# State-space layer of a hybrid encoder: phasor tables transposed to [state group, step], and the carry between runs worked out once for the two groups of a pair

## The chip, the cores and the metric

One core of one Trainium2 chip runs the whole kernel. The metric is the device time of one execution in microseconds (us), the median of three timed runs. A difference of about 0.2% (4.4 us here) is what a measurement of this kernel can tell from no change. The profile is of one more execution, taken by the hardware profiler.

## The reference, cut to what matters

The kernel computes one encoder layer of 2048 positions and 1024 channels: an input projection, three mixers side by side (state space, Fourier, windowed attention), an output projection, and a gated feed-forward part. The change lies in the state-space mixer alone:

```python
lam_bar = jnp.exp(lam * dt)                                  # per direction, group and state
b_bar = ((lam_bar - 1.0) / lam)[..., None] * b
for d, rev in ((0, False), (1, True)):
    bu = complex(einsum(u, b_bar[d].real), einsum(u, b_bar[d].imag))
    h[d] = associative_scan(a * left + right, (lam_bar[d], bu), reverse=rev, axis=1)
y = einsum(h.real, c_re) - einsum(h.imag, c_im) + d_skip * u
y = gelu(y); y = y * sigmoid(y @ w_glu)
```

There are 24 channel groups of 16 channels, each with 64 complex states and two directions.

## The kernel before, in words

**The state-space mixer.** Two groups make a pair, so there are 12 pairs. The sequence is cut into 256 blocks of 8 positions. Within a block the work is done by matmuls; across the 256 blocks a complex recurrence runs. It is made real by phasors: block values are rotated by the angle that has built up since the start of a *run* of 16 blocks, and then a real scan with the magnitudes (`rho`) suffices. So 256 blocks are 16 runs of 16 blocks, and 512 columns hold the two directions of a group. Real and imaginary parts lie in the two halves of the 128 partitions.

Four tables hold cosine and sine of the angles: `t1c` and `t1s` for the step inside a run, `t2c` and `t2s` for the run. `s5_consts` (L730) builds them as [16 steps, 48 columns], a column being one group and direction; `phasors` (L840) fills them by doubling, the first pair of tables on VectorE and the second on GpSimd. L832 multiplies the two sine tables by a sign. A multiplication of 512 columns by a table takes it with `bt(tsel(table))`: 16 entries for the inner dimension, 48 elements apart, used again for each of the 16 runs.

`s5_pair` (L861) prepares a pair: it builds matrices on VectorE (the first two pairs) or GpSimd, transposes them on TensorE, copies magnitudes into `RT` (L905), and puts two entries, one per group, into the queue `s5q`. `s5_chain` (L953) takes an entry and works it to the end. `N_CH` = 3 copies of it run at once, so three groups are in flight. Of one group it does:

1. two TensorE products into two PSUM banks `XA` and `XB` (fp32), a copy of magnitudes to `rx` on ScalarE (L979);
2. two multiplications of 128x512 by `t1c` and `t1s` (L980, L981), an addition, and a scan of 512 columns (L984);
3. the carry between runs (L986 to L1001) on 32 columns, the ends of the 32 runs: nine short VectorE instructions, among them a scan of 32 columns, and twice a TensorE product with the permutation `perm`, which swaps the halves of the partitions;
4. a second scan of 512 columns with the carries added in (L1002), two multiplications by the tables (L1003, L1004);
5. five TensorE products that make the output `y`, a ScalarE copy, and a DMA that stores it to `yd`.

When both groups of a pair are stored, its place among three prepared pairs (`N_SL`) comes free and `f_yd[b]` is set.

**What sets the order.** The program is written out by a planner (`Sched`, L121). Each part is a generator that asks for an engine with an estimated cost (`tt` at L277: 0.07 + 0.00105 per column, whatever the access pattern; `scan` at L302, `act` at L272, `mm` at L318). The planner always emits the instruction that can start earliest on its own clock, with a priority for ties. Each engine then runs its instructions strictly in the emitted order. Since all go through helpers, the profile's lines are those of the helpers: L277 two-operand arithmetic, L302 scans, L291 three-operand arithmetic, L318 matmuls, L272 ScalarE, L267 DMA. Parts outside the mixer are let in by futures: the Fourier weights by `f_yd[0]`, the preparation of the output weights by `f_yd[4]`, the remaining query tiles (`zrest`, 24 f16 matmuls of 128x512 each) by `f_yd[6]`, modulation rows (L446, L444) by `f_yd[7]`, gated linear unit and attention by `f_yd[10]`. The output projection needs all three mixers; the feed-forward part follows it.

Of the kernel before, what the change touches and what calls it, by code (L numbers as in the profile page):

```python
# [16 lines left out]
P = 128  # L17
# [26 lines left out]
S5_MUL = "V"  # L44
# [158 lines left out]
class Builder:  # L203
# [214 lines left out]
    def setup(self):  # L418
        A = self.A
        self.ones, self.ccol = self.const([P, P]), self.const([P, 8])  # L420
        self.bada, self.gains = self.const([P, 48]), self.const([P, 4, 8])
        yield from self.mset(0, self.ones, 1.0 / 1024)
        t = yield from self.dma(0, self.ccol, A["c_col"])
        t = yield from self.dma(0, self.bada, A["b_ada"])
        t = yield from self.dma(0, self.gains, A["gains"])
        self.f_cst.set(t)
        self.par, self.sgn = self.const([P, 3, 48]), self.const([P, 1])
# [302 lines left out]
    def s5_consts(self):  # L730
# [98 lines left out]
        for f in ends:  # L829
            t = max(t, (yield ("w", f)))  # L830
# [30 lines left out]
    def s5_pair(self, b, t, slots):  # L861
# [44 lines left out]
        left = [2, 0.0]  # L906
        for g in range(2):
            self.s5q.append((b, g, max(tp, tr), f_u, f_m, wt, U, RT, M0, Vf, Vs, left, slots))
            f, self.f_s5q = self.f_s5q, Fut()
            f.set(0)  # L910
        self.s5n -= 1
        if self.s5n == 0:
            self.f_s5q.set(0)
# [37 lines left out]
        done.set(t1)  # L951

    def s5_chain(self):  # L953
        PE = self.PE
        v4 = lambda a: a.rearrange("p (d a b) -> p d a b", d=2, a=16)
        v3 = lambda a: a.rearrange("p (d a) -> p d a", d=2)
        fl = lambda a: a.rearrange("p d a -> p (d a)")
        bt = lambda a: a.unsqueeze(2).to_broadcast([P, 2, 16, 16])
        M, ADD, SUB = ALU.mult, ALU.add, ALU.subtract
        while True:  # L960
            while not self.s5q:
                if self.s5n == 0:
                    return
                yield ("w", self.f_s5q)
            b, g, t, f_u, f_m, wt, U, RT, M0, Vf, Vs, left, slots = self.s5q.pop(0)
            t = max(t, (yield ("w", f_u)))
            s0 = 4 * b + 2 * g
            tsel = lambda tab: tab[:, :, s0:s0 + 2].rearrange("p b d -> p d b")
            tb_ = yield ("acq", self.bank["s"], 2)
            XA, XB = self.ps("s"), self.ps("s")  # L970
            rhs = (U[:, g, :], U[:, g, ::-1])
            ops = [(XX[:, d * 256:d * 256 + 256], wt[:, 2 * g + d, o:o + 128], rhs[d], True, True)
                   for XX, o in ((XA, 0), (XB, 64)) for d in range(2)]
            ta = yield from self.mm(max(t, tb_), ops[:2])
            tb = yield from self.mm(max(t, tb_), ops[2:])
            t12, rxs = self.u([2, 512]), self.u([768])
            gg, tt_ = t12[:, 0], t12[:, 1]
            rx, sc = rxs[:, 0:512], self.shape(rxs[:, 512:768], [8, 2, 16])
            tx = yield from self.act(t, v4(rx), bt(RT[:, 0, 2 * g:2 * g + 2]), AF.Copy)  # L979
# [3 lines left out]
            t = yield from self.tt(max(ta, tb), gg, gg, tt_, ADD, eng=S5_ADD)  # L983
            t = yield from self.scan(max(t, tx), tt_, rx, gg)  # L984

            pe_ = XA  # L986
            ends = v4(tt_)[:, :, :, 15]
            c2, s2 = tsel(self.t2c), tsel(self.t2s)
            tc_ = yield from self.tt(t, sc[:, 1], ends, c2, M)
            t = yield from self.mm(t, [(pe_[:, 0:32], self.perm, ends, True, True)])  # L990
            t = yield from self.tt(t, sc[:, 0], v3(pe_[:, 0:32]), s2, M)
            t = yield from self.tt(t, sc[:, 1], sc[:, 1], sc[:, 0], ADD)
            t = yield from self.scan(t, fl(sc[:, 2]), fl(RT[:, 1, 2 * g:2 * g + 2]), fl(sc[:, 1]))
            k1 = sc[:, 4, :, 1:16]
            tk = yield from self.tt(t, k1, sc[:, 2, :, 0:15], c2[:, :, 1:16], M)
            t = yield from self.mm(t, [(pe_[:, 64:96], self.perm, fl(sc[:, 2]), True, True)])
            t = yield from self.tt(t, sc[:, 3, :, 1:16], v3(pe_[:, 64:96])[:, :, 0:15], s2[:, :, 1:16], M)
            t = yield from self.tt(t, k1, k1, sc[:, 3, :, 1:16], SUB)
            t = yield from self.tt(t, k1, k1, self.rho[:, 0, s0:s0 + 2].unsqueeze(2).to_broadcast([P, 2, 15]), M)
            g4 = v4(gg)  # L1000
            t = yield from self.tt(t, g4[:, :, 1:16, 0], g4[:, :, 1:16, 0], k1, ADD)  # L1001
            t = yield from self.scan(t, tt_, rx, gg)  # L1002
            t1 = yield from self.tt(t, v4(rx), v4(tt_), bt(tsel(self.t1s)), M, eng=S5_MUL)  # L1003
            t = yield from self.tt(t, v4(gg), v4(tt_), bt(tsel(self.t1c)), M)  # L1004
            t = max(t, t1)
            tm = yield ("w", f_m)
            y = XA[:, 0:256]
            ops = [(y, M0[:, g, :], U[:, g, :], True, False)]
            for j, pp in ((0, gg), (1, rx)):
                ops.append((y[:, 1:256], Vf[:, 2 * g, 16:144] if j == 0 else Vs[:, 2 * g], pp[:, 0:255], False, False))  # L1010
                ops.append((y[:, 0:255], Vf[:, 2 * g + 1, 0:128] if j == 0 else Vs[:, 2 * g + 1],
                            pp[:, 256:511][:, ::-1], False, j == 1))
            t = yield from self.mm(max(t, tm), ops)
            t = yield from self.act(t, U[:, g], y, AF.Copy)
            self.free(t, XA)
            r = slice(16 * (2 * b + g), 16 * (2 * b + g) + 16)
            t = yield from self.dma(t, self.yd[r].rearrange("c t k -> t c k"), U[:, g])
            left[0] -= 1
            left[1] = max(left[1], t)
            if left[0] == 0:  # L1020
                slots.give(left[1])
                self.f_yd[b].set(left[1])


    def f_evac(self, t, ps, dst, done):
# [1088 lines left out]
```

## Time and profile before

| | |
|---|---|
| median of three runs | 2199.02 us (2198.71 to 2199.77) |
| the profiled execution | 2203.73 us, of which the span of instructions is 2202.0 us |
| mean granted TensorE clock | 0.955 |
| state-space stage: first table multiplication to last output | about 157 to 427 us |
| attention: first and last score row (L1327) | 500.2 and 870.1 us |

In the profile, PE is TensorE's matmul, PEld its weight load, DVE is VectorE, ACT ScalarE, POOL GpSimd and SP the queue from which DMAs are issued. A group's row gives line, engine, operation, output and inputs by name (`u` is any buffer in the chip's working memory, `ps` a PSUM bank, `c` a constant, `st` attention statistics), shapes, count, then busy time in us and mean duration of one in ns, then the engine's idle time just before them and what ended it. Durations of instructions that follow each other overlap a little, so a group's busy time is less than count times mean. A row of windows gives a stretch, its length, each engine's busy time with its count, then the granted TensorE clock, the DMA share and GB/s. A row of waits gives the waiting engine and line, what it waited for, the total in us, the number of times and the longest.

### The profile page before, as it was taken

How to read it: one execution, taken by the hardware profiler on the slowest of the kernel's cores; microseconds unless marked ns; L12 is line 12 of the kernel's file. 1: busy time of each engine (PE TensorE's matmuls, PEld its weight loads, DVE VectorE, ACT ScalarE, POOL GpSimd, SP SyncE). 2: the span in 40 equal slices, each digit the busy share in tenths (PEclk: the TensorE clock that was granted, in tenths of full speed). 3: DMA queues.
4: the chain of work that ended last, by engine and by line, in shares of the span. 5: the costliest groups of instructions: out<-in, count | busy, mean ns of one | idle time of the engine just before them, and what ended most of it. 6: DMA issues, size and time to landing. Idle time of an engine off the chain costs nothing.

```text
span 2202.0 us, 27575 instructions
## 1 busy us (share of the span) xinstructions
PE 2004.0 (91%) x10120; PEld 1001.0 (45%) x10120; DVE 1597.4 (73%) x2400; ACT 984.3 (45%) x1670; POOL 246.6 (11%) x310
## 2 busy tenths in 40 slices
PE   6778787889998858898999999999999999999997
PEld 2335565445454425443444444444444444444445
DVE  8999999886676584879988885565656665446456
ACT  3623233336576556556655553444444433222321
POOL 0565545020100000000000000000000000011002
PEclk9988898999999979799999999999999999999998
DMA  9351123673735273335655557565656494538533
GB/s 367 105 190 60 41 93 135 210 267 124 241 118 173 95 244 103 114 127 210 244 205 186 187 187 300 195 220 203 219 201 224 144 343 143 182 119 292 188 110 110
DMA packets 206667, 397.31 MB, mean 180 GB/s; under 512 B 19522, under 2 KB 111939, under 8 KB 206531
## 3 DMA queue, kind: packets, MB, share of 16 engines
q1 hardware_dynamic: 206530, 395.55, 52.2%
q8 instruction: 79, 1.29, 0.2%
q14 instruction: 58, 0.47, 0.1%
HBM read 258.93 MB, written 134.98 MB: 179 GB/s over the span
## 4 chain that ended last, share of the span: by engine, by line
PE 61%; DVE 25%; ACT 5%; issue 4%; DMA 3%; POOL 1%; SPq 1%; DVEq 0%; POOLq 0%; ACTq 0%
PE ps L318 61%; DVE u L277 12%; DVE u L291 8%; ACT u L272 5%; DVE u L302 2%; DVE u L446 1%; DMA u<-d 1%; POOL u L277 1%; SPq L267 1%; DMA u<-w_up 1%; DMA d<-u 1%; DVE u L284 0%; DVE u L410 0%; DMA u<-x 0%; DVE u L1327 0%
## 5 line engine op out<-in xcount | busy, mean ns | idle before, releaser
L318 PE MATMUL ps<-u,u 128*128 128x512 f16 (+9 forms) x9306 | 1918.7, 366 | 123.5 <-DVE u L277 35.7
L318 PEld LDWEIGHTS <-u 128*128 128x128 f16 (+1 forms) x9334 | 872.2, 101 | 1041.1 <-issue 174.5
L277 DVE TENSOR_TENSOR u<-u,u 128x512 f32<-128x512 f32 (+10 forms) x596 | 512.0, 892 | 107.0 <-ACT u L272 90.0
L272 ACT ACTIVATE u<-u 128x1024 f16<-128x1024 f32 (+8 forms) x483 | 403.2, 868 | 364.3 <-DVE u L277 158.8
L272 ACT ACTIVATE u<-ps 128x512 f32<-128x512 f32 (+6 forms) x511 | 276.3, 556 | 471.3 <-PE ps L318 445.7
L291 DVE SCALAR_TENSOR_TENSOR u<-u,c,u 128x1023 f32<-128x1023 f32 (+5 forms) x248 | 291.0, 1197 | 60.9 <-ACT u L272 55.2
L291 DVE SCALAR_TENSOR_TENSOR u<-ps,u 128x512 f32<-128x512 f32 (+3 forms) x231 | 152.4, 666 | 242.7 <-PE ps L318 201.1
L291 DVE SCALAR_TENSOR_TENSOR u<-u,u 128x1024 f16<-128x1024 f32 (+7 forms) x225 | 240.8, 1093 | 59.2 <-ACT u L272 55.8
L277 POOL TENSOR_TENSOR u<-u,u 128x288 f32<-128x288 f32 (+9 forms) x169 | 188.2, 1129 | 628.2 <-DVE u L291 459.1
L272 ACT ACTIVATE u<-u,c 128x1023 f32<-128x1023 f32 (+2 forms) x104 | 120.1, 1158 | 142.1 <-DVE u L291 122.0
L307 POOL MEMSET u<- 128x1 f32 x88 | 8.7, 99 | 1139.4 <-PE ps L318 510.9
L272 ACT ACTIVATE u<-u,st 128x384 f32<-128x384 f32 (+3 forms) x192 | 108.8, 596 | 35.6 <-DVE st L284 20.1
L318 PEld LDWEIGHTS ps<-u,u 128*128 128x128 f32 (+1 forms) x532 | 95.9, 194 | 62.3 <-DVE u L277 33.9
L277 DVE TENSOR_TENSOR u<-u 128x512 f32<-128x512 f32 (+8 forms) x184 | 92.3, 513 | 23.6 <-ACT u L272 22.4
L318 PE MATMUL ps<-u,c 128*128 128x32 f32 (+4 forms) x190 | 67.9, 465 | 43.7 <-DVE u L302 19.3
L318 PE MATMUL ps<-c,u 128*128 128x128 f16 (+1 forms) x568 | 61.9, 231 | 17.9 <-ACT u L272 11.4
L272 ACT ACTIVATE c<-u 128x2 f32<-128x2 f32 (+1 forms) x88 | 17.9, 203 | 130.3 <-DVE u L291 130.1
L1327 DVE CUSTOM_DVE_ANT_0 u<-ps,u 128x384 f32<-128x384 f32 (+1 forms) x96 | 49.1, 537 | 30.0 <-PE ps L318 29.3
L302 DVE TENSOR_TENSOR_SCAN u<-u,u 128x512 f32<-128x512 f32 (+1 forms) x72 | 68.9, 964 | 1.1 <-ACT u L272 0.9
L318 PEld LDWEIGHTS ps<-u,c 128*128 128x128 f32 (+1 forms) x190 | 30.7, 185 | 77.2 <-DVE u L302 29.7
L291 DVE SCALAR_TENSOR_TENSOR u<-u,st,u 128x384 f16<-128x384 f32 (+1 forms) x96 | 55.7, 609 | 11.9 <-ACT u L272 11.6
L277 DVE TENSOR_TENSOR u<-ps,u 128x512 f32<-128x512 f32 (+2 forms) x96 | 56.0, 600 | 7.6 <-PE ps L318 6.9
(52 smaller groups left out, 367.2 us busy)
## 6 DMA issues: line engine op xcount, KB each, us to landing
u<-d SPq DMA_DIRECT2D x226, 512.0 KB
d<-u SPq DMA_DIRECT2D x158, 512.0 KB
d<-u SPq DMA_DIRECT2D x111, 256.0 KB
u<-w_ada SPq DMA_DIRECT2D x48, 512.0 KB
u<-w_up SPq DMA_DIRECT2D x44, 512.0 KB
u<-d SPq DMA_DIRECT2D x66, 256.0 KB
u<-x SPq DMA_DIRECT2D x32, 512.0 KB
u<-d SPq DMA_DIRECT2D x24, 511.0 KB
```

The source lines that it names most:

```text
L267: self.SP.dma_start(out, in_)
L272: self.S.activation(out, in_, func, **kw)
L277: (self.V if eng == "V" else self.G).tensor_tensor(out, a, b, op)
L291: self.V.scalar_tensor_tensor(out, a, s, b, op0, op1)
L302: self.V.tensor_tensor_scan(out, d0, d1, 0.0, ALU.mult, ALU.add)
L307: (self.V if eng == "V" else self.G).memset(out, v)
L318: self.PE.matmul(o, a, b, start=st, stop=sp, skip_group_check=chain)
L446: V.tensor_tensor_reduce(out=w, in0=w, in1=self.crep, op0=ALU.mult, op1=ALU.add, scale=1.0, scalar=0.0, accum_out=mod[:, j:j + 1])
L1327: V.tensor_tensor_reduce(out=s_, in0=o, in1=self.bias[h // 2][:, h % 2, bo:bo + nk * 128], op0=ALU.add, op1=ALU.max, scale=1.0, scalar=-3e ...
```

## The change

It does four things. (1) Each of the four tables, once built, is copied by ScalarE into a new buffer [48 columns, 16 steps], so that the 16 entries of a run are adjacent; the sign of the sine tables goes into the scale of that copy, and the two VectorE sign multiplications of 768 columns are gone (a [128, 1] negation is new). (2) A queue entry is a pair: one chain does steps 1 and 2 for group 0 and then group 1, the carry (step 3) once for both on 64 columns, then steps 4 and 5 for each group. (3) There are two chains in place of three. (4) Both PSUM banks of a group come free after step 2; a third bank is taken for the carry's two products and for both groups' `y`. The numbers of matmuls, scans and multiplications of 512 columns are unchanged.

```diff
-N_CH = 3
+N_CH = 2
...
-        for ts_ in (t1s, t2s):
-            t = yield from self.ts(t, ts_, ts_, self.sgn, -1.0, M, M)
+        tn = yield from self.ts(0, self.nsg, self.sgn, -1.0, None, M)
+
+        byst = []
+        for f, (x, y) in zip(ends, ((t1c, t1s), (t2c, t2s))):
+            tf = yield ("w", f)
+            for src, sc in ((x, 1.0), (y, self.nsg)):
+                dst = self.u([48, 16])
+                t1 = yield from self.act(max(tf, tn), dst, src.rearrange("p j s -> p s j"), AF.Copy, scale=sc)
...
-        for g in range(2):
-            self.s5q.append((b, g, max(tp, tr), f_u, f_m, wt, U, RT, M0, Vf, Vs, left, slots))
+        self.s5q.append((b, max(tp, tr), f_u, f_m, wt, U, RT, M0, Vf, Vs, slots))
...
-            tsel = lambda tab: tab[:, :, s0:s0 + 2].rearrange("p b d -> p d b")
-            ta = yield from self.tt(ta, v4(gg), v4(XA), bt(tsel(self.t1c)), M)
-            tb = yield from self.tt(tb, v4(tt_), v4(XB), bt(tsel(self.t1s)), M)
-            self.free(tb, XB)
...
-            tc_ = yield from self.tt(t, sc[:, 1], ends, c2, M)
-            t = yield from self.mm(t, [(pe_[:, 0:32], self.perm, ends, True, True)])
...
+            gg, tt_, rx = (self.u([2, 512]) for _ in range(3))
+            sc = self.u([7, 4, 16])
+            tc, ts_, c2, s2 = (tab[:, 4 * b:4 * b + 4] for tab in (self.t1c, self.t1s, self.t2c, self.t2s))
+            for g in range(2):
+                ds = slice(2 * g, 2 * g + 2)
...
+                ta = yield from self.tt(ta, v4(gg[:, g]), v4(XA), bt(tc[:, ds]), M)
+                tb = yield from self.tt(tb, v4(tt_[:, g]), v4(XB), bt(ts_[:, ds]), M)
+                self.free(ta, XA)
+                self.free(tb, XB)
+                t = yield from self.tt(max(ta, tb), gg[:, g], gg[:, g], tt_[:, g], ADD, eng=S5_ADD)
+                t = yield from self.scan(max(t, tx), tt_[:, g], rx[:, g], gg[:, g])
+
+            tb_ = yield ("acq", self.bank["s"], 1)
+            pe_ = self.ps("s")
...
+            tc_ = yield from self.tt(t, sc[:, 1], ends, c2, M)
+            t = yield from self.mm(t, [(pe_[:, 0:64], self.perm, ends, True, True)])
...
+            for g in range(2):
+                t = yield from self.scan(tk, tt_[:, g], rx[:, g], gg[:, g])
+                t1 = yield from self.tt(t, v4(rx[:, g]), v4(tt_[:, g]), bt(ts_[:, ds]), M, eng=S5_MUL)
+                t = yield from self.tt(t, v4(gg[:, g]), v4(tt_[:, g]), bt(tc[:, ds]), M)
...
+                fs.append((yield from self.dma(t, self.yd[r].rearrange("c t k -> t c k"), U[:, g])))
+            self.free(t, pe_)
+            slots.give(max(fs))
```

The first place is VectorE's order in the middle of the stage. Before, `u_1736` and `u_1680` are the scratch buffers of two groups of different pairs in their carries, `u_89` and `u_90` the tables of the run, `u_1829` a third group in its first multiplications:

```order
L277 TENSOR_TENSOR u_1736<-ps_1717,u_90 128x32
L277 TENSOR_TENSOR u_1680<-ps_1666,u_90 128x2x15
L277 TENSOR_TENSOR u_1736<-u_1736 128x32
L277 TENSOR_TENSOR u_1671<-u_1671 16x2x16
L277 TENSOR_TENSOR u_1680<-u_1680 128x2x15
L302 SCALAR_TENSOR_TENSOR u_1736<-u_1531,u_1736 128x32
L291 SCALAR_TENSOR_TENSOR u_1368<-ps_1709,u_1368 64x2x64
L277 TENSOR_TENSOR u_1736<-u_1736,u_89 128x2x15
L277 TENSOR_TENSOR u_1680<-u_1680,c_82 128x2x15
L277 TENSOR_TENSOR u_1829<-ps_1806,u_88 128x512
L277 TENSOR_TENSOR u_1736<-ps_1717,u_90 128x2x15
L277 TENSOR_TENSOR u_1679<-u_1679,u_1680 128x2x15
```

In the changed program `u_1526` is the scratch buffer of a whole pair in its carry, `u_1020` and `u_1025` the transposed tables of the run, and `u_1688` and `u_1689` belong to the other chain's pair, in its first multiplications and scan:

```order
L302 SCALAR_TENSOR_TENSOR u_1526<-u_1400,u_1526 128x64
L277 TENSOR_TENSOR u_1413<-u_1413 16x2x16
L291 SCALAR_TENSOR_TENSOR u_1465<-ps_1466,u_1464 128x512
L277 TENSOR_TENSOR u_1526<-u_1526,u_1020 128x4x15
L277 TENSOR_TENSOR u_1688<-ps_1744,u_1007 128x512
L277 TENSOR_TENSOR u_1689<-ps_1745,u_1013 128x512
L277 TENSOR_TENSOR u_1526<-ps_1679,u_1025 128x4x15
L277 TENSOR_TENSOR u_1688<-u_1688,u_1689 128x512
L277 TENSOR_TENSOR u_1526<-u_1526 128x4x15
L302 SCALAR_TENSOR_TENSOR u_1689<-u_1690,u_1688 128x512
L277 TENSOR_TENSOR u_1526<-u_1526,c_82 128x4x15
L277 TENSOR_TENSOR u_1691<-u_1689,u_1020 128x64
```

The carry's instructions have 64 and 60 columns in place of 32 and 30, there are half as many, and those between them are the other chain's wide ones.

The second place is TensorE's order at the last output product of the last pair (the `y` of a group: a 128x256 and four 128x255 products). Before, `ps_3073` is that output and `ps_3200` a query tile:

```order
L318 MATMUL ps_3200<-u_194,u_1477 128x512
L318 MATMUL ps_3073<-u_3105,u_2669 128x255 x2
L318 MATMUL ps_3073<-u_3106,u_2668 128x255 x2
L318 LDWEIGHTS u_1477
L318 MATMUL ps_3200<-u_196,u_1477 128x512
```

In the changed program `ps_3273` is that output and `ps_3361` a tile of the Fourier mixer's channel transform:

```order
L318 MATMUL ps_3273<-u_2800,u_2801 128x256
L318 MATMUL ps_3273<-u_3121,u_2801 128x255 x2
L318 MATMUL ps_3273<-u_3123,u_2800 128x255 x2
L318 LDWEIGHTS u_2874
L318 MATMUL ps_3361<-u_1398,u_2874 128x128
```

Counted over the whole order ahead of this product, f16 matmuls of 128x512 are 488 before and 654 now, and those of 128x128 are 386 before and 416 now: 166 and 30 matmuls of other parts have moved ahead of the mixer's end. The carry's products ahead of it are 48 of 128x32 before and 24 of 128x64 now. Counted the same way on VectorE, ahead of the last scan (L302) there stand 18 modulation rows (L446) against 13, 23 three-operand instructions of 128x1024 (L291) against 18, 11 two-operand ones of 128x1024 (L277) against 7, four of 128x1023 against none, and 14 three-operand ones of 128x512 out of PSUM against 12.

More of the change, by code (lines that the diff above doesn't have):

```diff
@@ L982, in s5_chain @@
-            self.free(tb, XB)
[L983 to L988, printed above, removed]
+            b, t, f_u, f_m, wt, U, RT, M0, Vf, Vs, slots = self.s5q.pop(0)
+            t0 = max(t, (yield ("w", f_u)))
+            gg, tt_, rx = (self.u([2, 512]) for _ in range(3))
+            sc = self.u([7, 4, 16])
@@ new lines, in s5_chain @@
+            tc, ts_, c2, s2 = (tab[:, 4 * b:4 * b + 4] for tab in (self.t1c, self.t1s, self.t2c, self.t2s))
+            fs = []
+            for g in range(2):
+                ds = slice(2 * g, 2 * g + 2)
+                tb_ = yield ("acq", self.bank["s"], 2)
+                XA, XB = self.ps("s"), self.ps("s")
+                rhs = (U[:, g, :], U[:, g, ::-1])
+                ops = [(XX[:, d * 256:d * 256 + 256], wt[:, 2 * g + d, o:o + 128], rhs[d], True, True)
+                       for XX, o in ((XA, 0), (XB, 64)) for d in range(2)]
+                ta = yield from self.mm(max(t0, tb_), ops[:2])
+                tb = yield from self.mm(max(t0, tb_), ops[2:])
+                tx = yield from self.act(t0, v4(rx[:, g]), bt(RT[:, 0, ds]), AF.Copy)
+                ta = yield from self.tt(ta, v4(gg[:, g]), v4(XA), bt(tc[:, ds]), M)
[4 more added lines that the diff above has]
+                t = yield from self.scan(max(t, tx), tt_[:, g], rx[:, g], gg[:, g])
@@ L989, in s5_chain @@
+            tb_ = yield ("acq", self.bank["s"], 1)
+            pe_ = self.ps("s")
+            t = max(t, tb_)
+            ends = tt_.rearrange("p g (d a b) -> p (g d) a b", d=2, a=16)[:, :, :, 15]
             tc_ = yield from self.tt(t, sc[:, 1], ends, c2, M)
[L990 to L991 removed]
+            t = yield from self.mm(t, [(pe_[:, 0:64], self.perm, ends, True, True)])
@@ L1013, in s5_chain @@
[L1013 to L1022, printed above, removed]
+            t = yield from self.tt(t, k1, k1, self.rho[:, 0, 4 * b:4 * b + 4].unsqueeze(2).to_broadcast([P, 4, 15]), M)
@@ new lines, in s5_chain @@
+            first = gg.rearrange("p g (d a b) -> p (g d) a b", d=2, a=16)[:, :, 1:16, 0]
+            tk = yield from self.tt(t, first, first, k1, ADD)
+            tm = yield ("w", f_m)
+            for g in range(2):
+                ds = slice(2 * g, 2 * g + 2)
+                t = yield from self.scan(tk, tt_[:, g], rx[:, g], gg[:, g])
+                t1 = yield from self.tt(t, v4(rx[:, g]), v4(tt_[:, g]), bt(ts_[:, ds]), M, eng=S5_MUL)
+                t = yield from self.tt(t, v4(gg[:, g]), v4(tt_[:, g]), bt(tc[:, ds]), M)
+                t = max(t, t1)
+                y = pe_[:, 256 * g:256 * g + 256]
+                ops = [(y, M0[:, g, :], U[:, g, :], True, False)]
+                for j, pp in ((0, gg[:, g]), (1, rx[:, g])):
+                    ops.append((y[:, 1:256], Vf[:, 2 * g, 16:144] if j == 0 else Vs[:, 2 * g], pp[:, 0:255], False, False))
+                    ops.append((y[:, 0:255], Vf[:, 2 * g + 1, 0:128] if j == 0 else Vs[:, 2 * g + 1],
+                                pp[:, 256:511][:, ::-1], False, j == 1))
+                t = yield from self.mm(max(t, tm), ops)
+                t = yield from self.act(t, U[:, g], y, AF.Copy)
+                r = slice(16 * (2 * b + g), 16 * (2 * b + g) + 16)
+                fs.append((yield from self.dma(t, self.yd[r].rearrange("c t k -> t c k"), U[:, g])))
```

53 lines of the change are left out of this document (13 added, 40 removed).

## The prediction

> **What bounds the kernel now.** I read the page first, for the engines' shares and the slices, then windows that follow the stages, then the waits and the groups of the state-space stage. The page's PE row, and of its 40 slices (55 us each) PE, DVE and the granted clock:
>
> ```profile
> PE 2004.0 (91%) x10120; PEld 1001.0 (45%) x10120; DVE 1597.4 (73%) x2400; ACT 984.3 (45%) x1670; POOL 246.6 (11%) x310
> PE   6778787889998858898999999999999999999997
> DVE  8999999886676584879988885565656665446456
> PEclk9988898999999979799999999999999999999998
> ```
>
> TensorE sets the time over most of the span; only in the first eight slices or so is VectorE at 8 or 9 while PE is at 6 to 8. The windows say the same by stage (ahead of the state-space stage; the stage; three later ones):
>
> ```profile
> 100.00:157.00 57.00, 46.10 (x186) 19.66 (x186) 55.03 (x100) 19.48 (x31) 38.92 (x37) 0.88 0.61 202
> 157.00:427.00 270.00, 214.52 (x1204) 155.33 (x1203) 256.79 (x487) 83.34 (x174) 121.75 (x126) 0.90 0.30 95
> 500.00:600.00 100.00, 96.39 (x650) 51.65 (x649) 66.34 (x182) 53.67 (x139) 6.69 (x5) 0.98 0.50 165
> 700.00:900.00 200.00, 155.34 (x981) 86.64 (x979) 125.02 (x256) 119.75 (x248) 0.00 (x0) 0.87 0.41 136
> 1130.00:2202.00 1072.00, 1046.59 (x4942) 484.19 (x4941) 671.01 (x725) 421.44 (x636) 32.56 (x86) 0.99 0.57 198
> ```
>
> In the stage VectorE is busy 256.8 of 270 us (95%), PE 214.5 (79%), so PE idles 55.5 us. From 1130 us on PE is 98% busy: nothing that VectorE saves there shortens the end. What the change can win is therefore PE's idle time in the stage, and PE work itself. The waits of PE there:
>
> ```profile
> PE ps L318 <- DVE u L277: 25.4, 19, 3.0
> PE ps L318 <- DVE u L302: 19.3, 20, 2.8
> PE ps L896 <- DVE u L277: 2.1, 3, 1.1
> ```
>
> The 19.3 us behind L302 (scans) are the permutation product waiting for the scan ahead of it. The 27.5 us behind L277 are mostly output products that wait for the last multiplications. The remaining 55.5 − 19.3 − 27.5 = 8.7 us have other causes.
>
> **The tables.** VectorE's wide groups in the stage; the fifth row is of the whole run, a three-operand instruction of the same 128x512 with one input in PSUM and one in working memory, both read in plain order:
>
> ```profile
> L302 DVE TENSOR_TENSOR_SCAN u<-u,u 128x512 f32<-128x512 f32 x48 | 61.7, 1286 | 1.1 <-ACT u L272 0.9
> L277 DVE TENSOR_TENSOR u<-u,u 128x512 f32<-128x512 f32 x48 | 53.2, 1144 | 0.1
> L277 DVE TENSOR_TENSOR u<-ps,u 128x512 f32<-128x512 f32 x48 | 47.9, 1010 | 2.1 <-PE ps L318 1.6 <-DMA d<-u 0.4
> L277 DVE TENSOR_TENSOR u<-u 128x512 f32<-128x512 f32 x24 | 19.0, 794 | 0.1
> ...
> L291 DVE SCALAR_TENSOR_TENSOR u<-ps,u 128x512 f32<-128x512 f32 x179 | 122.3, 688 | 217.9 <-PE ps L318 201.1 <-ACT u L272 14.5 <-DMA u<-d 2.0
> ```
>
> The multiplications that read a table cost 1.010 us (from PSUM) and 1.144 us (from working memory); plain reads of that size cost 0.688 and 0.794 us (the in-place addition). If the stride alone is the difference, adjacent entries save 48 × (1.010 − 0.688) = 15.5 us and 48 × (1.144 − 0.794) = 16.8 us, together 32.3 us of VectorE. It could also be the repetition of 16 entries that costs, and then nothing is saved. Two rows decide between the ends:
>
> ```profile
> L277 DVE TENSOR_TENSOR u<-u,u 128x256 f32<-128x256 f32 x8 | 2.8, 417 | 0.0
> L277 DVE TENSOR_TENSOR u<-u 128x256 f32<-128x256 f32 x4 | 1.5, 417 | 0.0
> ```
>
> The eight are L889 and L890 for the two pairs built on VectorE: one input is 16 adjacent entries, repeated eight times, the form that the change gives the tables. They cost 417 ns, as the plain sums of the same size do. So repetition is free where the entries are adjacent, and I take all 32.3 us (bounds 0 and 32.3).
>
> **The carry.** Its nine short instructions per group, eight rows:
>
> ```profile
> L277 DVE TENSOR_TENSOR u<-u,u 128x30 f32<-128x30 f32 x48 | 14.9, 314 | 0.2
> L277 DVE TENSOR_TENSOR u<-u,u 128x32 f32<-128x32 f32 x24 | 8.0, 334 | 0.1
> L277 DVE TENSOR_TENSOR u<-u 128x32 f32<-128x32 f32 x24 | 7.7, 321 | 0.0
> L302 DVE TENSOR_TENSOR_SCAN u<-u,u 128x32 f32<-128x32 f32 x24 | 7.7, 320 | 0.0
> L277 DVE TENSOR_TENSOR u<-u 128x30 f32<-128x30 f32 x24 | 7.4, 310 | 0.1
> L277 DVE TENSOR_TENSOR u<-u,c 128x30 f32<-128x30 f32 x24 | 7.0, 297 | 0.1
> L277 DVE TENSOR_TENSOR u<-ps,u 128x32 f32<-128x32 f32 x24 | 4.5, 189 | 1.9 <-PE ps L318 1.8
> L277 DVE TENSOR_TENSOR u<-ps,u 128x30 f32<-128x30 f32 x24 | 4.5, 189 | 3.6 <-PE ps L318 3.5
> ```
>
> They sum to 61.7 us for 216 instructions. The change runs 108 of twice the width. A column costs (688 − 417)/256 = 1.06 ns, so 32 more cost 34 ns: 30.9 + 108 × 0.034 = 34.5 us, a saving of 27.1. That is the upper end. The rows hold a warning: from PSUM such an instruction takes 189 ns, with both inputs in working memory about 314. GpSimd is busy 121.75 us of the stage (window row), and that work stays. If the surplus, 168 × 0.125 = 21.0 us, is time spent behind GpSimd, halving the number need not halve it; if half of it falls on other instructions, 10.5 us come back and 16.6 are saved. I take 16.6, the lower end.
>
> [...]
>
> VectorE's content of the stage falls from 256.8 to 256.8 − 32.3 − 16.6 = 207.9 us.
>
> **Other edits of VectorE, ScalarE and PSUM.**
>
> ```profile
> L286 DVE TENSOR_SCALAR u<-u,c 128x768 f32<-128x768 f32 x2 | 1.2, 616 | 0.0
> L272 ACT ACTIVATE u<-u 128x1024 f32<-128x1024 f32 x4 | 4.2, 1056 | 4.2 <-DMA u<-d 4.1
> 130.83 1.22 POOL L277 TENSOR_TENSOR u<-u,u 128x336 f32<-128x336 f32 x1
> ```
>
> The two sign multiplications go, ahead of the stage, where VectorE is busy 55.0 of 57 us: −1.2 us. ScalarE's four copies of 768 columns cost at most 1.06 us each. The second tables are done at 130.83 + 1.22 = 132.05 us and first used after 157, and ScalarE idles 37.5 of those 57 us: priced at nothing; uncovered they cost 4.2. No PE wait names a bank, so the third bank is priced at nothing too.
>
> **TensorE.**
>
> ```profile
> L318 PE MATMUL ps<-u,u 128*128 128x512 f16 x148 | 37.7, 388 | 0.3 <-ACT u L272 0.3
> L318 PE MATMUL ps<-u,u 128*128 128x128 f16 x384 | 32.4, 244 | 0.0
> L318 PE MATMUL ps<-u,c 128*128 128x32 f32 x96 | 18.8, 288 | 19.5 <-DVE u L302 19.3
> ```
>
> The last row is 48 permutation products in two records each, 18.8/48 = 0.39 us apiece. 24 go, −9.4; 24 grow by 32 columns, about +0.7: −8.7 us. The order also puts 166 more 128x512 f16 matmuls and 30 more 128x128 ahead of the stage's last matmul: 166 × 37.7/148 + 30 × 32.4/384 = 42.3 + 2.5 = 44.8 us. They are moved, not added, and fill PE where it waited.
>
> PE's idle time: 24 handoffs from scan to permutation product remain of 48, so 19.3 becomes 9.7. VectorE moves 25.3 us of other work forward too:
>
> ```profile
> L446 DVE CUSTOM_DVE_ANT_0 u<-u,u 128x1024 f32<-128x1024 f32 x32 | 39.2, 1231 | 1.2 <-DMA u<-w_ada 1.2
> L291 DVE SCALAR_TENSOR_TENSOR u<-u,u 128x1024 f16<-128x1024 f32 x126 | 154.4, 1239 | 52.5 <-ACT u L272 52.0
> L277 DVE TENSOR_TENSOR u<-u,u 128x1024 f16<-128x1024 f32 x106 | 130.2, 1251 | 73.4 <-ACT u L272 72.2 <-POOL u L286 0.9
> L277 DVE TENSOR_TENSOR u<-u,u 128x1023 f32<-128x1023 f32 x4 | 6.5, 1636 | 0.0
> ```
>
> Five of the first, five of the second, four of each of the others and two of 0.688 us: 6.2 + 6.2 + 5.0 + 6.5 + 1.4 = 25.3, so VectorE needs 233 us against PE's 214.5 + 44.8 − 8.7 = 250.6. VectorE no longer sets the pace, but an output product still waits for its own multiplication. I let the 27.5 us fall to half, 13.8 (bounds 0 and 27.5), and keep the 8.7. PE idles 9.7 + 13.8 + 8.7 = 32.2 instead of 55.5: −23.3 us. The last pair now runs alone at the end; the 44.8 us of moved matmuls stand beside it, so I add nothing, and the slower rival prices it without that cover.
>
> **Sum.** −23.3 (idle) − 8.7 (permutation products) − 1.2 (signs) = −33.2 us. The profiled execution took 2203.7 us, of which the span is 2202.0; it becomes 2170.5. The median of the runs is 2199.0, 4.7 us under it; the same saving gives 2165.8, forecast **2166 us**. With 13.8 either way its own range is 2152 to 2180.
>
> **Rivals.**
>
> *The clock rises too: 2154.* The windows pair PE's busy share with the clock: 78% and 0.87, 79% and 0.90, 96% and 0.98, 98% and 0.99. At 250.6/(250.6 + 32.2) = 89% busy, a line through them gives 0.945, and 250.6 × (1 − 0.90/0.945) = 11.9 us go besides. With still less idling 2140 is reached. Against it: the stage keeps its many short waits, which may be what holds the clock down. [...]
>
> *The handoffs stay exposed: 2187 (2180 to 2196).* Two chains, each with a carry for a whole pair, offer VectorE less to choose from than three. If the waits behind multiplications stay at 27.5 and those behind scans too, of 19.3, what is left is the 8.7 + 1.2 = 9.9 us of work: 2189; with a little of the waits gone 2187. For it: these waits are of dependence as much as of load. Against: the order puts the other chain's wide instructions between the carry's.
>
> *The tables bring nothing: 2179.* If repetition costs, not the stride, VectorE stays at 95% and only 9.7 + 8.7 + 1.2 = 19.6 go. The 417 ns rows speak against it.
>
> *Slower: 2223.* Both chains reach their carries together. A carry is nine dependent VectorE instructions, by the rows 2.59 us, and two products of 0.39: 3.4 us in which PE has none of the mixer's work. Exposed for eleven pairs that is 37 us. Add the last pair alone: per group 2 × 0.688 + 0.794 + 2 × 1.286 + 2 × 0.794 = 6.33, twice, and a carry, 16.1 us. With 27.5 + 8.7 kept, PE idles 89.7 instead of 55.5, +34.2, less the 9.9: +24.3. It decides once PE idles more than 55.5 + 9.9 = 65.4 us over the stage's work. For it: the order puts the last two pairs before the final one in lockstep. Against: the preparation of later pairs and 166 moved matmuls lie between.
>
> **How the numbers follow.** Forecast 0.45, clock 0.22, exposed handoffs 0.17, tables 0.05, slower 0.11. About 0.2% (4.4 us) is what a measurement of this kernel can tell from no change. Faster holds the forecast, the clock, the tables and 0.12 of the handoffs: 0.84; the other 0.05 of the handoffs is the same; slower is 0.11. The range 2140 to 2190 reaches from the clock's better end to the middle of the exposed handoffs and leaves out about 0.2.
>
> **What would show it.** Right: 48 multiplications from PSUM near 0.69 us and 48 from working memory near 0.79; twelve of each carry row, of 64 or 60 columns, their sum between 34 and 45 us; 48 records of the permutation product; VectorE below 90% busy up to the last wide scan, PE near 89% there; waits of PE behind L302 near 10 us and behind L277 near 14. A clock of 0.94 or more in the stage shows the first rival. Multiplications still near 1.0 and 1.1 us show the tables' case. Waits that stay at 45 us or more show the exposed handoffs; PE idle over 65 us, in gaps that lie in the carries and at the last pair, the slower one. If the stage gains 33 us and the end doesn't move, the later stages were not bound by TensorE, and the sum is wrong there.

## The result, and the profile after

The changed kernel takes 2170.73 us (median of four runs, 2169.49 to 2172.28), the kernel before 2198.86 us: a ratio of 0.9873, 95% interval 0.9856 to 0.989. It is 28.1 us faster; the forecast was 33.2 faster, 2166.

First the page after: the engines' shares, and of the 40 slices PE, VectorE and the granted clock.

```profile
PE 1967.2 (91%) x10072; PEld 983.4 (45%) x10072; DVE 1553.1 (72%) x2291; ACT 1001.9 (46%) x1682; POOL 247.6 (11%) x310
...
PE   5788888789999549998999999999999999999996
...
DVE  8999898858665764899988884666665664547356
...
PEclk9989999899999769999999999999999999999998
```

The span of the profiled execution fell from 2202.0 to 2169.7 us, by 32.3. TensorE's busy time fell by more than that, from 2004.0 to 1967.2, by 36.8; its idle time over the whole span is 2169.7 − 1967.2 = 202.5 us and was 198.0. So over the whole span the time came out of TensorE's work and not out of its waiting, which is the reverse of the forecast's sum. By stretches the waiting did change: PE's idle time is 42.0 us ahead of the stage (39.9 before), 46.4 in it (55.5) and 114.1 behind it (102.6). The window of the stage after, and the waits of PE and of VectorE's multiplications in it:

```profile
157.00:435.00 278.00, 231.64 (x1359) 160.02 (x1357) 243.85 (x422) 94.93 (x193) 129.89 (x126) 0.93 0.40 130
```

```profile
DVE u L277 <- PE ps L318: 21.2, 15, 3.2
PE ps L318 <- DVE u L302: 20.0, 9, 7.0
PE ps L318 <- DVE u L277: 13.9, 11, 2.9
...
PE ps L901 <- DVE u L277: 5.8, 1, 5.8
```

VectorE was 95% busy in the stage and is now busy 243.9 of 278 us, 88%; its multiplications now wait 21.2 us for TensorE (6.9 before). PE idles 278.0 − 231.6 = 46.4 us, where it was 55.5. The waits behind scans (L302) are fewer, 9 instead of 20, but their sum did not halve: it is 20.0 us, since each is longer. VectorE's groups that the change touches:

```profile
L277 DVE TENSOR_TENSOR u<-u,u 128x512 f32<-128x512 f32 x72 | 56.7, 814 | 0.3
L277 DVE TENSOR_TENSOR u<-ps,u 128x512 f32<-128x512 f32 x48 | 31.7, 677 | 13.5 <-PE ps L318 13.3
...
L277 DVE TENSOR_TENSOR u<-u,u 128x60 f32<-128x60 f32 x24 | 8.0, 338 | 0.3
...
L302 DVE TENSOR_TENSOR_SCAN u<-u,u 128x64 f32<-128x64 f32 x12 | 5.2, 429 | 0.1
...
L277 DVE TENSOR_TENSOR u<-u,c 128x60 f32<-128x60 f32 x12 | 3.9, 333 | 0.1
L277 DVE TENSOR_TENSOR u<-u 128x64 f32<-128x64 f32 x12 | 3.6, 304 | 0.1
L277 DVE TENSOR_TENSOR u<-u,u 128x64 f32<-128x64 f32 x12 | 3.6, 297 | 0.1
...
L277 DVE TENSOR_TENSOR u<-u 128x60 f32<-128x60 f32 x12 | 3.0, 257 | 0.2
...
L277 DVE TENSOR_TENSOR u<-ps,u 128x60 f32<-128x60 f32 x12 | 2.6, 214 | 7.1 <-PE ps L318 7.1
L277 DVE TENSOR_TENSOR u<-ps,u 128x64 f32<-128x64 f32 x12 | 2.5, 212 | 0.8 <-PE ps L318 0.8
```

The first row now holds the 48 multiplications and the 24 additions together. Multiplications and additions took 53.2 + 47.9 + 19.0 = 120.1 us before and take 56.7 + 31.7 = 88.4: 31.7 less. The carry's eight rows sum to 32.4 us; they were 61.7. TensorE's groups in the stage:

```profile
L318 PE MATMUL ps<-u,u 128*128 128x256 f32 x240 | 63.7, 395 | 1.3 <-ACT u L272 1.3
L318 PE MATMUL ps<-u,u 128*128 128x255 f32 x192 | 48.4, 396 | 13.9 <-DVE u L277 13.9
L318 PE MATMUL ps<-u,u 128*128 128x128 f16 x480 | 33.1, 228 | 0.8 <-DVE u L291 0.8
...
L318 PE MATMUL ps<-u,c 128*128 128x64 f32 x48 | 10.4, 308 | 20.7 <-DVE u L302 20.0 <-PE ps L318 0.7
```

The permutation products cost 10.4 instead of 18.8 us, 8.4 less. The other 28.4 of the 36.8 us lie in matmuls whose number did not change: the same 240 products of 256 columns took 71.8 us before and take 63.7. Lastly the end of the stage, a part of PE's timeline while the twelfth pair is alone (in brackets the idle time before a row and what ended it):

```profile
395.80 7.10 PE L318 MATMUL ps<-u,u 128*128 128x512 f16 x41
409.94 0.66 PE L318 MATMUL ps<-u,c 128*128 128x64 f32 x2 [7.04 <-DVE u L302]
410.96 1.44 PE L318 MATMUL ps<-u,u 128*128 128x512 f16 x3 [0.36 <-DVE u L291]
413.23 0.59 PE L318 MATMUL ps<-u,u 128*128 128x512 f16 x2 [0.83 <-DVE u L291]
416.40 2.72 PE L318 MATMUL ps<-u,u 128*128 128x512 f16 x6 [2.58 <-DVE u L291]
```

The matmuls that were to cover the last pair are nearly used up; PE waits 7.04 + 0.36 + 0.83 + 2.58 = 10.8 us in these 23 us.

### The profile page after: what moved, and what is told of

Read it like the earlier page. It is cut to its first block, busy times and chain, and to the rows that moved or that the text cites. A ratio compares the mean times of both kernels' runs of the same rounds, so it can differ in the third digit from the quotient of the medians.

```text
span 2169.7 us, 27415 instructions
## 1 busy us (share of the span) xinstructions
PE 1967.2 (91%) x10072; PEld 983.4 (45%) x10072; DVE 1553.1 (72%) x2291; ACT 1001.9 (46%) x1682; POOL 247.6 (11%) x310
## 4 chain that ended last, share of the span: by engine, by line
PE 64%; DVE 22%; ACT 5%; issue 4%; DMA 4%; SPq 1%; POOL 1%; DVEq 0%; POOLq 0%; ACTq 0%
PE ps L318 64%; DVE u L277 10%; DVE u L291 8%; ACT u L272 4%; DVE u L302 2%; SPq L267 1%; DMA u<-w_in 1%; DMA u<-d 1%; DVE u L1332 1%; DMA d<-u 1%; DVE u L446 0%; POOL u L277 0%; DMA u<-w_ada 0%; POOL u L286 0%; DVE u L410 0%
## 5 line engine op out<-in xcount | busy, mean ns | idle before, releaser
L318 PE MATMUL ps<-u,u 128*128 128x512 f16 (+10 forms) x9306 | 1886.9, 362 | 101.3 <-DVE u L291 41.1
L277 DVE TENSOR_TENSOR u<-u,u 128x512 f32<-128x512 f32 (+11 forms) x584 | 508.2, 903 | 103.1 <-ACT u L272 88.4
L272 ACT ACTIVATE u<-u 128x1024 f16<-128x1024 f32 (+7 forms) x485 | 406.1, 869 | 374.8 <-DVE u L277 165.7
L272 ACT ACTIVATE u<-ps 128x512 f32<-128x512 f32 (+7 forms) x511 | 276.6, 555 | 406.2 <-PE ps L318 371.5
L291 DVE SCALAR_TENSOR_TENSOR u<-u,c,u 128x1023 f32<-128x1023 f32 (+5 forms) x248 | 291.2, 1196 | 59.7 <-ACT u L272 52.8
L291 DVE SCALAR_TENSOR_TENSOR u<-ps,u 128x512 f32<-128x512 f32 (+4 forms) x231 | 152.0, 665 | 246.4 <-PE ps L318 195.8
L291 DVE SCALAR_TENSOR_TENSOR u<-u,u 128x1024 f16<-128x1024 f32 (+6 forms) x225 | 240.3, 1091 | 57.4 <-ACT u L272 53.7
L277 POOL TENSOR_TENSOR u<-u,u 128x288 f32<-128x288 f32 (+9 forms) x169 | 189.8, 1137 | 608.8 <-DVE u L291 460.9
L272 ACT ACTIVATE u<-u,c 128x1023 f32<-128x1023 f32 (+3 forms) x106 | 123.4, 1165 | 141.9 <-DVE u L291 122.1
L318 PE MATMUL ps<-u,c 128*128 128x512 f32 (+4 forms) x142 | 57.8, 523 | 57.3 <-DVE u L277 22.9
L318 PEld LDWEIGHTS ps<-u,u 128*128 128x128 f32 (+1 forms) x532 | 89.9, 178 | 40.0 <-DVE u L277 18.8
L318 PE MATMUL ps<-c,u 128*128 128x128 f16 (+1 forms) x568 | 61.0, 231 | 26.5 <-ACT u L272 21.2
L277 DVE TENSOR_TENSOR u<-u 128x512 f32<-128x512 f32 (+8 forms) x136 | 67.2, 498 | 16.9 <-ACT u L272 15.3
L291 DVE SCALAR_TENSOR_TENSOR u<-u,st,u 128x384 f16<-128x384 f32 (+1 forms) x96 | 55.3, 601 | 17.5 <-ACT u L272 17.1
L302 DVE TENSOR_TENSOR_SCAN u<-u,u 128x512 f32<-128x512 f32 (+1 forms) x60 | 67.0, 1124 | 0.5
L272 ACT ACTIVATE u<-u,c,c 128x512 f32<-128x512 f32 (+1 forms) x64 | 48.9, 804 | 25.5 <-DVE u L277 9.5
```

Source lines behind the costliest of these rows:

```text
L272: self.S.activation(out, in_, func, **kw)
L277: (self.V if eng == "V" else self.G).tensor_tensor(out, a, b, op)
L291: self.V.scalar_tensor_tensor(out, a, s, b, op0, op1)
L302: self.V.tensor_tensor_scan(out, d0, d1, 0.0, ALU.mult, ALU.add)
L318: self.PE.matmul(o, a, b, start=st, stop=sp, skip_group_check=chain)
```

## The experiments

Two theories stood at the start. *VectorE's pace*: the gain follows the VectorE time that is saved, so tables and carry share it. *Handoffs*: TensorE waits on a chain of dependent steps, so the halved carry and the number of chains count. A third came up on the way, *later order*: what the planner moved out of attention decides. All medians and ratios are against the kernel before on the same chip:

| kernel | median us | ratio (95%) |
|---|---|---|
| tables alone, three chains of a group | 2170.0 | 0.9877 (0.9859 to 0.9895) |
| changed kernel, tables not transposed | 2192.2 | 0.9972 (0.9962 to 0.9983) |
| before, two chains of a group | 2217.5 | 1.0087 (1.0065 to 1.0109) |
| tables, two chains of a group | 2184.1 | 0.9933 (0.9916 to 0.9949) |
| changed kernel, three chains of a pair | 2191.1 | 0.9963 (0.995 to 0.9976) |
| changed kernel, third chain for the last pair | 2197.5 | 0.9998 (0.9988 to 1.0007) |
| changed kernel, attention behind the projection | 2272.1 | 1.0335 (1.0314 to 1.0356) |
| both of these | 2274.7 | 1.0348 (1.0329 to 1.0367) |
| changed kernel, planner costs times 0.75 | 2172.7 | 0.9879 (0.9864 to 0.9894) |
| the same, three chains of a pair | 2169.4 | 0.9864 (0.9849 to 0.9879) |
| the same costs, two chains, tables not transposed | 2195.4 | 0.9977 (0.9966 to 0.9989) |
| changed kernel, four prepared pairs | 2183.4 | 0.9928 (0.9913 to 0.9943) |

### The tables, alone and taken back

```diff
-        for ts_ in (t1s, t2s):
-            t = yield from self.ts(t, ts_, ts_, self.sgn, -1.0, M, M)
+                dst = self.u([48, 16])
+                t1 = yield from self.act(max(tf, tn), dst, src.rearrange("p j s -> p s j"), AF.Copy, scale=sc)
...
-            tsel = lambda tab: tab[:, :, s0:s0 + 2].rearrange("p b d -> p d b")
+            tsel = lambda tab: tab[:, s0:s0 + 2]
```

> The kernel before with the transposed tables alone: carry per group, three chains. VectorE's pace: the gain of 28.1 us (2198.9 to 2170.7) goes with the VectorE time that each part saves in the profile after, 31.7 us by the tables and 29.3 by the carry, so the tables bring 52% of it, 14.6 us: 2184. Handoffs: TensorE waits on the chain of one group, not on VectorE's load, so its waits behind scans (19.3) and multiplications (27.5) stay: 2194 to 2199. Both expect the multiplications at about 0.68 us from PSUM and 0.80 from working memory.

Measured: 2170.0 us, the whole gain of the change from the first of its four parts. Shown are the page's engines, the window of its stage (last output product at 391.3 us, in the kernel before at 426.9), PE's waits there, and the groups that answer to those above. The profiled execution (span 2163.2) is the fastest of this kernel's runs, which reach from 2164.9 to 2172.5 us, so its times lie about 5 us under the median:

```profile
PE 1982.0 (92%) x10120; PEld 988.3 (46%) x10120; DVE 1566.0 (72%) x2399; ACT 990.2 (46%) x1674; POOL 248.5 (11%) x310
```

```profile
157.00:392.00 235.00, 197.28 (x1209) 143.73 (x1208) 224.06 (x487) 84.39 (x176) 125.02 (x122) 0.97 0.35 110
```

```profile
PE ps L318 <- DVE u L277: 14.7, 13, 2.5
PE ps L318 <- DVE u L302: 13.4, 16, 2.3
```

```profile
L277 DVE TENSOR_TENSOR u<-u,u 128x512 f32<-128x512 f32 x48 | 38.8, 844 | 0.1
L277 DVE TENSOR_TENSOR u<-ps,u 128x512 f32<-128x512 f32 x48 | 31.9, 676 | 1.0 <-PE ps L318 0.7
```

```profile
L318 PE MATMUL ps<-u,u 128*128 128x256 f32 x240 | 65.5, 396 | 3.0 <-DVE u L277 2.9
L318 PE MATMUL ps<-u,u 128*128 128x255 f32 x192 | 51.1, 413 | 10.8 <-DVE u L277 9.8 <-DVE u L307 0.9
```

The multiplications save (53.2 − 38.8) + (47.9 − 31.9) = 30.4 us, and the window that held the stage is 35 us shorter (270 to 235). VectorE is 224.1 of 235 us busy, 95% as before: it set the pace of the stage with three chains, and what it was relieved of came off the stage. For PE the shorter window is 37.7 us of idle time instead of 55.5 and 197.3 us of work instead of 214.5. The granted clock in the stage is 0.97 and was 0.90, and PE's busy time over the run fell by 2004.0 − 1982.0 = 22.0 us though its 10120 matmuls are all there. Both theories' numbers were wrong: the pace was right in kind, but tables alone were not half of the gain, they were all of it.

The other way round, the changed kernel with tables that are copied but stand as before; every engine has the same instructions in the same order:

```diff
-                dst = self.u([48, 16])
+                dst = self.u([16, 48])
...
-            tc, ts_, c2, s2 = (tab[:, 4 * b:4 * b + 4] for tab in (self.t1c, self.t1s, self.t2c, self.t2s))
+            tc, ts_, c2, s2 = (tab[:, :, 4 * b:4 * b + 4].rearrange("p j s -> p s j") for tab in (self.t1c, self.t1s, self.t2c, self.t2s))
```

> The changed kernel with the tables copied but not transposed: the same instructions in the same order on every engine, only the 16 entries stand 48 elements apart again. VectorE's pace: the multiplications go back to 1.01 and 1.14 us, 31.7 us more of VectorE, and half of the gain goes: 2171 + 14.6 = 2185. Handoffs: the order and the halved carry hold the gain, 2171 to 2176. If stride is not what costs, the multiplications stay at 0.68 and 0.80.

Measured: 2192.2, 21.5 us over the changed kernel. Its groups of wide two-operand arithmetic on VectorE:

```profile
L277 DVE TENSOR_TENSOR u<-u,u 128x512 f32<-128x512 f32 x72 | 70.7, 1009 | 0.3
...
L277 DVE TENSOR_TENSOR u<-ps,u 128x512 f32<-128x512 f32 x48 | 47.7, 1017 | 12.5 <-PE ps L318 12.4
```

From 677 back to 1017 ns with nothing but the stride changed: the stride is the price, as the forecast argued, and not the repetition. Since every order is the same, these two profiles also show how the stride reaches the time: PE is busy 13.3 us longer (1980.5 against 1967.2) and idles 8.8 us more (211.3 against 202.5). What is left of the change without the transposed tables, the pair's carry, two chains and the earlier release of PSUM banks, gains 0.28% (0.9972), 6 us. The release of the banks was not tried by itself.

### The number of chains, and what the pair's carry is worth

Two edits: `N_CH` from 3 to 2 in the kernel before, and in the tables-alone kernel.

> The kernel before with two chains of one group in place of three. VectorE's pace: VectorE was 95% busy with three and has the same 256.8 us to do with two, so little changes if two still fill it: 2199 to 2205. Handoffs: with a chain fewer in flight the carries and the waits lie open, 24 carries of 3.4 us of which a third or more shows: 2225 or more.

> Transposed tables, carry per group, two chains of one group (the tables-alone kernel with a chain fewer). The transposed tables are worth what they were with three chains, 29 us, and the lost chain costs what it cost with the old tables, 18 us: 2217 - 29 = 2188, so that the pair's carry is worth the 17 us to the changed kernel's 2171. Rival: with VectorE relieved two chains fill it less and the lost chain costs more, 2195 or over; or the carry of a pair is worth nothing, 2171.

Measured: 2217.5 us, between the two theories' ranges, and 2184.1. A chain fewer costs 18 us with the old tables and 14 with the new. PE's waits in the stage of the second kernel:

```profile
PE ps L318 <- DVE u L302: 27.4, 22, 4.2
PE ps L318 <- DVE u L277: 21.6, 14, 3.4
```

With two chains the waits behind scans are 27.4 us instead of 13.4 with three. The changed kernel has 20.0 and is 13 us faster than this one (25 with the old tables: 2192.2 against 2217.5). So the pair's carry is worth something: with two chains it takes back what the lost chain cost, and with the new tables the two together come to nothing. The forecast took the halved carry off the waits that three chains leave, and counted the lost chain only in two of its rivals.

### Three chains of a pair, and the last pair

`N_CH` = 3 in the changed kernel; and, in another, a third chain that takes the twelfth pair only:

```diff
-    def s5_chain(self):
+    def s5_chain(self, mine):
...
-            while not self.s5q:
+            while not [q for q in self.s5q if q[0] in mine]:
...
-        for _ in range(N_CH):
-            sp(self.s5_chain(), 1, S5_B)
+        for mine in (range(11), range(11), (11,)):
+            sp(self.s5_chain(mine), 1, S5_B)
```

> The changed kernel with three chains of a pair. Last pair alone: with two chains the twelfth pair has the engines to itself, priced at 16.1 us of VectorE's steps; with three it runs beside the two ahead of it: 2155 to 2163. Rival, preparation: GpSimd's building of the matrices and the four PSUM banks set how many pairs are in flight, so a third chain waits and nothing changes: 2168 to 2174.

> The changed kernel with a third chain that takes the twelfth pair alone, so that it runs beside the tenth and eleventh. Last pair alone: its 16 us or so come back, 2152 to 2161. Rival, later order: what follows the stage decides, as with three chains of a pair, which ended the stage 31 us sooner and took 20 us longer: with 747 wide f16 matmuls between the first and the last attention score instead of 761, nothing is gained, 2171 to 2180.

Measured: 2191.1 and 2197.5 us, 20 and 27 over the changed kernel. Neither theory of the stage explains that, and the stage isn't where it happens: the last output product ends at 403.8 and 412.9 us, in the changed kernel at 434.9. With the third chain for the last pair PE's waits in the stage are shorter:

```profile
PE ps L318 <- DVE u L277: 15.9, 12, 3.4
PE ps L318 <- DVE u L302: 12.6, 8, 5.2
```

The waits behind scans fall from 20.0 to 12.6 us, as the last pair alone would have it. But attention takes longer. Its score rows, first and last start in us, of the changed kernel, of three chains of a pair and of the third chain for the last pair:

```profile
L1332 DVE CUSTOM_DVE_ANT_0 u<-ps,u x96: 414/553/559, 461.2 to 856.1; 128x384 f32<-128x384 f32 x84, 128x256 f32<-128x256 f32 x12
```

```profile
L1332 DVE CUSTOM_DVE_ANT_0 u<-ps,u x96: 416/553/560, 451.9 to 873.0; 128x384 f32<-128x384 f32 x84, 128x256 f32<-128x256 f32 x12
```

```profile
L1332 DVE CUSTOM_DVE_ANT_0 u<-ps,u x96: 417/552/561, 460.2 to 880.3; 128x384 f32<-128x384 f32 x84, 128x256 f32<-128x256 f32 x12
```

394.9 us becomes 421.1 and 420.1; before it was 369.9 (500.2 to 870.1). The instructions are the same, but the planner, whose clock the chains change, had put other work among the scores. So a program that wins in the stage can lose it behind the stage, and the third theory was formed.

### The order behind the stage

First attempt: `P_ATT` from 0.5 to 3, which ranks attention behind the output projection and packs more matmuls among its scores; alone, and with the third chain for the last pair.

> The changed kernel with the planner's priority of attention set behind the output projection's (0.5 becomes 3): the state-space stage keeps its order, and 941 wide f16 matmuls stand between the first and the last attention score instead of 761 (879 in the kernel before). Later order: TensorE's idle time in that stretch, 65.7 us after and 46.7 before, falls to 50 or less, and the time to 2150 to 2160. Rival: attention is a chain of dependent steps that its lower rank only stretches: 2171 to 2185.

> Both: the third chain for the twelfth pair, and attention behind the output projection (903 wide f16 matmuls between the scores). If the lead that the stage wins is lost only at its end and in attention, the lead of about 45 us at 420 us stays: 2150 to 2157. Rival: the lead is lost wherever VectorE and ScalarE have to catch up, whatever the order: 2165 to 2175.

Measured: 2272.1 and 2274.7 us. The score rows of the first:

```profile
L1332 DVE CUSTOM_DVE_ANT_0 u<-ps,u x96: 408/552/559, 458.4 to 959.3; 128x384 f32<-128x384 f32 x84, 128x256 f32<-128x256 f32 x12
```

Attention takes 500.9 us instead of 394.9, and the time grows by 101: the rival had the direction, a lower rank only stretches the chain, but expected 2185 at most. The count of matmuls among the scores doesn't tell how good an order is.

Second attempt: leave ranks alone, and make the planner's clock run through the stage as it did before, by taking 0.75 of the cost it plans for VectorE's steps in a chain:

```diff
+    def tt5(self, t, out, a, b, op, eng="V"):
+        t = yield (eng, 0.75 * (0.07 + 0.00105 * cols(out)), t)
+        self.V.tensor_tensor(out, a, b, op)
+        return t + self.LAT
...
-                t = yield from self.scan(max(t, tx), tt_[:, g], rx[:, g], gg[:, g])
+                t = yield from self.scan5(max(t, tx), tt_[:, g], rx[:, g], gg[:, g])
```

> The changed kernel with the planner's costs of VectorE's steps in a chain times 0.75; nothing else. The planner then ends the stage earlier on its own clock and puts 879 wide f16 matmuls between the first and the last attention score, as in the kernel before (761 after), and 485 instead of 665 ahead of the stage's last product. Later order: the lead won in the stage is kept, TensorE idles under 50 us in attention (65.7 after): 2150 to 2160. Rival: the stage itself gets a worse order, since the real steps cost more than the planner thinks: 2165 to 2175.

> Lowered planner costs and three chains of a pair; 459 wide f16 matmuls ahead of the stage's last product, 879 between the scores. If three chains lost their 20 us to the later order alone, they are now as fast as two chains with lowered costs or some us faster, since the last pair isn't alone: 2146 to 2158. If three chains crowd the stage, they stay slower than two by 5 us or more.

> Lowered planner costs, the pair's carry and two chains, with tables that are not transposed: the same order on every engine as the lowered costs with transposed tables. The tables are worth what they were in other pairs of kernels, 21 to 29 us: slower by that. Against the kernel before, whose later order it shares, it shows what the pair's carry and two chains are worth by themselves: 10 to 22 us if the 17 us between two chains of a group and two of a pair come from there, nothing (2195 to 2203) if the pair's carry only moves waits.

> The changed kernel with four prepared pairs in place of three; 569 wide f16 matmuls ahead of the stage's last product, 879 between the scores. Later order: as with the planner's costs lowered, 2150 to 2162. Rival: the stage's own order is what the two-chain program lives from, and its last pair alone stays: 2168 to 2173.

Measured: 2172.7, 2169.4, 2195.4 and 2183.4 us. With as many wide matmuls among the scores as before (879), and score rows that take 370.2 us again (469.4 to 839.6), two chains of a pair are no faster than the changed kernel (0.9879 against 0.9873), as the rival had it. PE idles 18.3 us less (184.2 against 202.5) but is busy 17.6 us longer. The lowered costs also change the order in the stage, so what the later order costs the changed kernel by itself stays open; on balance nothing is gained. From three chains of a pair the order did take the 20 us: 2191.1 with the plain costs, 2169.4 with the lowered ones (expected were 2146 to 2158), while PE's idle time falls from 204.6 to 187.5 us. The tables are worth 22.7 us here (2195.4 to 2172.7), as between the other two-chain pairs of kernels. The pair's carry without them gains 0.23% (0.9977), 5 us, and with them nothing against tables alone (2170.0). The profile of the three chains of a pair with lowered costs, its engines and PE's waits in the stage (L963 are the scans there, L958 the multiplications):

```profile
PE 1977.8 (91%) x10072; PEld 985.2 (46%) x10072; DVE 1558.3 (72%) x2291; ACT 989.4 (46%) x1674; POOL 248.1 (11%) x310
```

```profile
PE ps L318 <- DVE u L963: 20.6, 15, 3.4
PE ps L318 <- DVE u L958: 15.9, 10, 3.1
```

Against the tables-alone kernel PE's busy time is 1982.0 − 1977.8 = 4.2 us less, and the waits behind scans are 20.6 against 13.4 us, 7.2 more. So also with three chains and a like order behind the stage a pair's carry is paid for in waits: its one permutation product stands behind the scans of both groups. That this is why is read from the program, not tried by itself. Four prepared pairs gained nothing (2183.4, outside both expectations). The score rows take 367.5 us there but start at 483.6 instead of 461.2; why the kernel is 13 us slower than with three was not followed up.

## Why the prediction came out, point by point

The time (2170.7 for 2166, inside 2152 to 2180) was right; how it was made up was only half right, and to that extent the hit was luck.

**The tables: right.** "Together 32.3 us of VectorE": 31.7. The 417 ns rows did tell the price of a repeated read. ScalarE's copies take 1.53 and 1.63 us each, more than the "at most 1.06" of the forecast, but they stayed hidden: the first wide scan starts at 161.5 us in both traces. By the same number the sign multiplications brought nothing (forecast −1.2).

**The carry on VectorE: mis-sized.** "I take 16.6, the lower end": 61.7 − 32.4 = 29.3 us, over even the upper end of 27.1, and the rows' sum lies under the forecast's 34 to 45, since a row of 64 columns costs little more than one of 32 (the multiplications from PSUM 212 against 189 ns). Little of the waiting that the forecast put down to GpSimd moved in the changed kernel: the copies of magnitudes (24 of 128x60) take 313 ns instead of 289. The surplus of the short rows with both inputs in working memory, 338 against 214 ns, is still there per instruction. For wide rows the traces show that it comes with GpSimd's work: plain 128x512 rows with both inputs in working memory took 794 ns in the stage (GpSimd busy 121.75 of 270 us; the twelve of them beside a GpSimd instruction 911, the other twelve 679), but 690 between 600 and 870 us, where GpSimd is busy 0.00 us, and 688 out of PSUM. The 16.6 let half of the surplus fall on other instructions; that is not borne out here.

**VectorE no longer sets the pace: right.** It is 88% busy in the stage and waits 21.2 us for TensorE.

**The failed step: "24 handoffs from scan to permutation product remain of 48, so 19.3 becomes 9.7".** They are 20.0. The forecast counted handoffs as if each kept its length; with two chains each is longer (27.4 us for 22 waits in the kernel of two chains of a group), and the pair's carry brings that down only to 20.0. Of these, 7.04 us are the single wait of the last pair. That step is the one under "The last pair now runs alone at the end; the 44.8 us of moved matmuls stand beside it, so I add nothing": nearly all of the moved matmuls were done by 403 us, and PE waited 10.8 us beside the last pair. So PE idles 46.4 us in the stage and not 32.2, a miss of 14.2, and is 83% busy there and not 89%. Behind the stage, where the sum had no term, it idles 11.5 us more than before, so that over the whole run it idles 4.5 us more and not 23.3 less. The rival "the handoffs stay exposed" was half right: the waits behind scans stayed (20.0 for 19.3), those behind multiplications fell to 13.9 + 5.8 = 19.7 from 27.5, and its sign of 45 us or more for both was not reached (39.7).

**What stood in its place: mostly the clock.** The products went from 18.8 to 10.4 (−8.4, forecast −8.7; for its +0.7 for wider products it names no row, and 48 records of 308 instead of 288 ns make about 1.0), and the rest of PE's busy time fell by 28.4 us. In these traces the granted clock is at every moment either full or half, and f16 matmuls of 128x512 in a row start 216 ns apart at full and 427 ns apart at half clock. So PE's work at half clock can be counted: 143.2 us before, 99.2 in the changed kernel. Half of the difference, about 22 us, is what the clock gave (an estimate from these two numbers); about 6 of the 28.4 stay open.

In the stage the count fell from 50.5 to 31.0, worth about 9.7 us, close to the 11.9 of the rival "the clock rises too", though its sign, 0.94 or more in the stage, was just missed (0.93). Behind the stage it fell from 69.1 to 46.0, about 11.6 us, and the added idle time of 11.5 us takes that back.

The tables-alone kernel shows the clock by itself: no matmul fewer, the clock 0.97 instead of 0.90 in the stage, the 256-column products 396 instead of 424 ns, 101.3 us of PE's work at half clock, so about 21 of the 22.0 us that PE is busy less. And with nothing but the stride put back, PE's work at half clock rises from 99.2 to 129.1 us. Fewer and shorter waits of PE (13.4 us in 16 and 14.7 in 13, for 19.3 in 20 and 25.4 in 19) stand beside the higher clock; what in them moves it, no run shows.

**So the sum held by two errors.** The forecast had −23.3 of idle time and −8.7 of products; measured in the two profiled executions are +4.5 of idle time, −8.4 of products and −28.4 of other matmul time, −32.3 together. In the stage alone it is −9.1 of idle time, −8.4 of products and about −9.7 by the clock, and these three make most of the −32.3. And it gave the carry a share: undone singly, the tables are the whole gain.

**The slower rival** named a mechanism that is there, dependent carries in few chains: without the tables the changed kernel gains 6 us, and two chains of a group lose 18. Its point of decision, 65.4 us of idle time, wasn't reached (46.4).

**Which version is best.** Tables alone (2170.0), the changed kernel (2170.7) and three chains of a pair with lowered costs (2169.4) are the same within their intervals; no run beat the changed kernel by what can be measured.

## What to carry to other kernels

Where an engine is 95% busy in a stage, look at its widest instructions first: here the time taken from them came off the stage, and four transposed tables, made by hidden copies, brought the whole gain. A change that saves instructions and also takes away a chain in flight must be priced against waits of the new length, not the old length times the new count. In a planned program a win in one stage can be lost in the next one through the order alone, so count by stage and look at the stretch behind it.

## What the runs showed that had not been expected

TensorE's busy time is no fixed cost: with the same 10120 matmuls it is 22.0 us smaller when VectorE lets it wait less in the stage, because less of the work falls into stretches of half clock (101.3 us instead of 143.2), and a product of 256 columns takes 396 ns instead of 424. For VectorE, doubling a carry's row from 32 to 64 columns costs 23 ns from PSUM (189 to 212), nothing for an addition or a multiplication with both inputs in working memory (321 to 304 ns, 334 to 297), and 109 ns for the scan (320 to 429): so, but for the scan, most of the price of such an instruction here is paid per instruction and not per column.
